# The second attention of a two-layer trunk: TensorE put in the order of the source

## The chip, the cores and the metric

The kernel runs on one core of one Trainium2 chip. The core has a matrix engine (TensorE, PE in the profile; its weight loads are listed apart as PEld), a vector engine (VectorE, DVE), a scalar engine (ScalarE, ACT), a general engine (GpSimd, POOL) and a queue engine that issues transfers (SyncE, SP). Each engine takes its instructions in its own order, and semaphores make one wait for another. The metric is the device time of one execution in microseconds (us).

## The reference, cut to what matters

The model has two layers over 512 latent tokens and 256 context tokens, of width 1024. The change is in the attention of the second layer, which has 16 query heads of 64 columns, 4 key and value heads, a band of 128 tokens to either side, all context keys, and one learned sink logit per head that takes part in the softmax but has no value:

```
q_x, k_x, v_x = jnp.split(h_x @ w_in, [C_Q_COLS, C_Q_COLS + C_KV_COLS], axis=-1)
q_x = apply_rope(heads(q_x, GQA_HEADS), cos, sin)
...
s = jnp.einsum('bqkgd,bnkd->bkgqn', qg, k).astype(jnp.float32) * (HEAD_DIM ** -0.5)
s = jnp.where(mask, s, NEG_INF)
p = jax.nn.softmax(jnp.concatenate([s, sink], axis=-1), axis=-1)[..., :-1]
o = jnp.einsum('bkgqn,bnkd->bqkgd', p.astype(v.dtype), v)
...
out_x = block_sweep(blk, q_x).reshape(B, S, C_Q_COLS) @ w_out
```

In this layer only the latent tokens have queries. After it come the second feed-forward block and a last norm.

## The kernel before

Activations lie transposed: 1024 columns as eight tiles of 128 rows (hb in the profile), each as a high and a low part, so that one product of full precision is three matmuls: high weight by high input, high by low, low by high (`mm3`, lines 207 to 209). A projection of 128 output columns for 512 tokens is therefore 8 x 3 = 24 matmuls of 128x512. Weights come from memory as 128x1024 tiles (raw) and are split: ACT makes the high part (wh, line 158), DVE the low part (wl, line 159).

The stage of the change runs in this order of the source. First the keys of two heads for the latent tokens (`k_x(0)`, 24 matmuls of 128x512), whose inputs the norm has just been making one tile after the other (DVE lines 353 and 355, ACT line 354); then the norm of the context tokens, which begins with two small matmuls (line 312); the values in three groups (`v_part`, lines 432 to 434: 144 matmuls of 128x256); the context keys, the second pair of key heads, and the first query projection. A query projection ends with the rotation of positions (`rope_of`): DVE shuffles and multiplies (lines 386 and 387), POOL multiplies and adds (388 and 389), ACT and DVE write the two parts of gq (369 and 372).

Then come 32 steps: eight pairs of heads m, each with four blocks i of 128 queries. A step has two functions. `a` does the scores: eight matmuls (1540 and 1542) into two buffers s of PSUM, one for each head of the pair, and there are only these two; DVE adds the mask and finds the extreme (1544); ACT exponentiates (1549, with the sum of the row) and takes the exponential of the sink, one head at a time (1551); DVE adds and inverts (1553 and 1554); POOL scales p (1557). `b` turns p by 8 or 10 transposes on TensorE (1569 and 1581), copies them into one buffer pt (ACT 1577 and 1582, DVE 1575), and after every second step does the values of two blocks at once (line 411, ten matmuls that must stay together) and splits their result. `run_steps` calls a of step n, then b of step n-1, then the extra work ("fillers") of step n: the seven query projections that are left, and the half of the output projection that needs the first eight heads only (eight pieces of 12 matmuls, one for each 128 columns of the output). Both have the one PSUM buffer lin. A table says which steps have them: two whole projections in the four steps of m = 0 and of m = 1, one in those of m = 2, 3 and 4, two pieces of the output projection at m = 5, four at m = 6, two at m = 7.

This order of the source is not the order on the engines. A scheduler of the framework reorders every engine's queue when the program is built, by its own costs; only groups marked as unbroken stay together.

After the 32 steps, the other half of the output projection follows (t from lines 207 to 209), and the norm for the feed-forward block.

Of the kernel before, what the change touches and what calls it, by code (L numbers as in the profile page):

```python
# [17 lines left out]
KT = D // P  # L18
# [19 lines left out]
def tile_trunk(  # L38
# [1414 lines left out]
    with ExitStack() as st:  # L1453
# [22 lines left out]

        def k_x(i, w):
# [14 lines left out]

        w0 = [wslice(t) for t in S.next()]
# [14 lines left out]
        def q_piece(m):  # L1508
            def f():
                wh, wl = (wslice(t) for t in S.next())  # L1510
                ps = linp() if m else tp()
                mm3(ps, wh, wl, xh, xl)
                q_tile(m, ps)
            return f
# [10 lines left out]
        def gqa_step(m, i):  # L1525
# [5 lines left out]
            def a():  # L1531
# [4 lines left out]
                for c in range(2):  # L1536
# [13 lines left out]
                    sk = 2 * m + c  # L1550
                    nc.scalar.activation(es[:, c : c + 1], snk[:, sk : sk + 1], AF.Exp, bias=mx[:, c : c + 1], scale=-1.0)
                    pp.append(p)
                nc.vector.tensor_add(rs, rs, es)
# [6 lines left out]
            def b():  # L1560
# [41 lines left out]
            return a, b  # L1602
# [4 lines left out]
        def wo1(m, w, c0, n, k0):  # L1607
            wh, wl = wo_slices(w, m % 2)
            ps = tp() if k0 else linp()
            cs = slice(c0, c0 + n)  # L1610
            if k0:
                before[0] = mm3(ps[:, 0:n], wh, wl, lambda k: hx[k0 + k][:, 0, cs], lambda k: hx[k0 + k][:, 1, cs], 4)
            else:
                mm3(ps.rearrange("p (a n) -> p a n", a=2), wh, wl, lambda k: att(k)[0], lambda k: att(k)[1], 4)
            gate = mod[1][:, 2, 0, m : m + 1]
            if k0 == 0:
                x1[m] = xr[m]
            nc.vector.scalar_tensor_tensor(x1[m][:, cs], ps[:, 0:n], gate, x1[m][:, cs], op0=ALU.mult, op1=ALU.add)

        def first_part(t):  # L1620
            d = {}

            def f(m):
                if m % 2 == 0:
                    d["w"] = S.next()
                wo1(m, d["w"], 0, NX, 0)

            return [lambda m=m: f(m) for m in (2 * t, 2 * t + 1)]

        for m in range(KT):  # L1630
# [3 lines left out]
        q_piece(0)()  # L1634
        steps, fillers = [], []
        plan = {
            0: [q_piece(1), q_piece(2)], 1: [q_piece(3), q_piece(4)], 2: [q_piece(5)], 3: [q_piece(6)], 4: [q_piece(7)],
            5: first_part(0), 6: first_part(1) + first_part(2), 7: first_part(3),
        }
        for m in range(8):  # L1640
            steps += [gqa_step(m, i) for i in range(4)]
            fillers += spread(plan[m], 4)
        run_steps(steps, fillers)
        held = []
        for t in range(4):
            w = S.next(0 if t >= 2 else 2)
            for m in (2 * t, 2 * t + 1):
                if t == 0:
                    wo1(m, w, 0, NX, 4)
                else:  # L1650
                    wo1(m, w, 0, 256, 4)
                    held.append((m, w))
# [3 lines left out]
        sums = sq_sum([x1[k][:, halves[0]] for k in range(KT)], npool)  # L1656
        for m, w in held[:1]:
            wo1(m, w, 256, 256, 4)
# [3 lines left out]
        for m, w in held[1:]:  # L1662
            wo1(m, w, 256, 256, 4)
# [319 lines left out]
```

## Time and profile before

| what | us |
| --- | --- |
| three runs of the kernel | 1601.09, 1604.99, 1609.46 |
| their median | 1604.99 |
| span of the profiled execution | 1606.8 |
| keys, values and first query projection in it | 990.4 to 1033.3 |
| first scores to the last values in it | 1039.4 to 1216.6 |
| TensorE busy in the span | 1541.8 |
| VectorE busy in the span | 1242.9 |

For the profiled execution only its span is given, 1606.8 us; it lies between the runs' lowest and highest time, 1.8 us above their median. In the rows of a timeline the first number is the start in us from the span's beginning, the second the duration. Matmuls overlap in the pipe: the time that one takes from its neighbours is the distance between two starts and not its duration, and "busy" counts the duration.

### The profile page before, as it was taken

Reading aid. Unit: us, or ns where it says so; the run is one execution under the profiler, and the core shown is the slowest. Engines: PE = TensorE matmul, PEld = TensorE weight load, DVE = VectorE, ACT = ScalarE, POOL = GpSimd, SP = SyncE. Lnnn points to the kernel's source line nnn. Section 1 sums busy time; section 2 is a strip of 40 time slices with the busy share of each in tenths; the row PEclk is TensorE's granted clock in tenths of the full one; section 3 lists DMA queues with packets and bytes.
Section 4 is the critical chain, followed back from the end, with each engine's and each line's share of the span. In section 5 each row is a group of like instructions: output and inputs, shape, how many; then the busy total and the mean of one; then the engine's idle time right before and its main releaser. Section 6 shows DMA issues by size and latency. Waiting matters only on the chain.

```text
span 1606.8 us, 25479 instructions
## 1 busy us (share of the span) xinstructions
PE 1541.8 (96%) x9854; PEld 1377.4 (86%) x9854; DVE 1242.9 (77%) x2125; ACT 734.1 (46%) x1276; POOL 275.9 (17%) x311
## 2 busy tenths in 40 slices
PE   5899999999999999999999999999998999999997
PEld 3798888877878998999999998886777899989897
DVE  4667798966698789879798867677766987869686
ACT  4346545445344413434424254466664543525354
POOL 2222223463010000010100001354331000000001
PEclk9999999999999999999999999999999999999999
DMA  9312354543145465485866652320011442423321
GB/s 348 100 53 70 99 157 136 182 128 101 63 132 158 118 173 155 133 221 154 213 183 162 201 146 71 106 66 27 15 40 54 131 144 68 131 72 100 118 80 53
DMA packets 68577, 195.28 MB, mean 122 GB/s; under 512 B 6772, under 2 KB 19220, under 8 KB 68456
## 3 DMA queue, kind: packets, MB, share of 16 engines
q1 hardware_dynamic: 58824, 161.26, 31.5%
q0 software_dynamic: 9056, 31.87, 9.4%
q8 instruction: 78, 1.28, 0.3%
q10 hardware_dynamic: 576, 0.52, 0.1%
q14 instruction: 43, 0.35, 0.1%
HBM read 160.45 MB, written 4.86 MB: 103 GB/s over the span
## 4 chain that ended last, share of the span: by engine, by line
PE 52%; DVE 5%; DMA 4%; issue 4%; ACT 1%; POOL 0%; DVEq 0%; POOLq 0%; ACTq 0%; SPq 0%
PE f L1764 4%; PE f L1763 4%; PE f L1762 4%; PE f L1334 4%; PE f L1333 4%; PE f L1332 4%; PE f L1374 3%; PE f L1375 3%; PE f L1373 3%; PE t L411 2%; PE f L1815 2%; PE f L1817 2%; PE f L1816 2%; DMA wl<-raw 2%; PE t L1569 2%
## 5 line engine op out<-in xcount | busy, mean ns | idle before, releaser
L196 ACT ACTIVATE wh<-raw 128x1024 fp32r<-128x1024 f32 (+1 forms) x96 | 92.3, 978 | 232.4 <-DVE raw L540 106.6
L207 PE MATMUL lin<-hb,wh 128*128 128x512 f32 (+1 forms) x456 | 162.1, 356 | 8.3 <-DVE rbuf L387 2.1
L208 PE MATMUL lin<-hb,wh 128*128 128x512 f32 (+1 forms) x456 | 160.3, 351 | 1.0 <-DVE hb L1106 0.7
L209 PE MATMUL lin<-hb,wl 128*128 128x512 f32 (+1 forms) x456 | 158.4, 347 | 0.0
L197 DVE TENSOR_TENSOR wl<-raw,wh 128x1024 fp32r<-128x1024 f32 (+1 forms) x96 | 107.1, 1122 | 36.3 <-ACT wh L196 34.3
L269 DVE SCALAR_TENSOR_TENSOR junk<-raw,tables 128x1024 bf16<-128x1024 f32 x80 | 98.6, 1233 | 19.2 <-DMA raw<-in_ada_wT_dram 18.7
L202 POOL DMA_DIRECT2D wl<-raw x39 | 34.0, 872 | 445.3 <-ACT wl L201 412.0
L207 PEld LDWEIGHTS lin<-hb,wh 128*128 128x128 f32 x456 | 86.3, 189 | 23.9 <-issue 2.8
L1373 PE MATMUL f<-g,wh 128*128 128x512 f32 (+1 forms) x304 | 103.0, 340 | 0.6 <-DVE s L1362 0.6
L1374 PE MATMUL f<-g,wh 128*128 128x512 f32 (+1 forms) x304 | 102.9, 339 | 0.0
L1763 PE MATMUL f<-hb,wh 128*128 128x256 f32 x360 | 101.8, 284 | 0.0
L1762 PE MATMUL f<-hb,wh 128*128 128x256 f32 x360 | 101.6, 283 | 0.0
L1764 PE MATMUL f<-hb,wl 128*128 128x256 f32 x360 | 101.4, 284 | 0.0
L1375 PE MATMUL f<-g,wl 128*128 128x256 f32 (+1 forms) x304 | 100.8, 337 | 0.0
L1334 PE MATMUL f<-hb,wl 128*128 128x384 f32 x288 | 96.5, 335 | 1.0 <-DMA wl<-raw 1.0
L208 PEld LDWEIGHTS lin<-hb,wh 128*128 128x128 f32 x456 | 86.5, 190 | 12.4 <-DVE hb L1106 1.4
L159 DVE TENSOR_TENSOR wl<-raw,wh 128x1024 fp32r<-128x1024 f32 x61 | 80.7, 1325 | 20.6 <-ACT wh L158 20.3
L1332 PE MATMUL f<-hb,wh 128*128 128x384 f32 x288 | 96.4, 335 | 0.0
L1333 PE MATMUL f<-hb,wh 128*128 128x384 f32 x288 | 96.4, 335 | 0.0
L209 PEld LDWEIGHTS lin<-hb,wl 128*128 128x128 f32 x456 | 86.5, 190 | 10.8
L158 ACT CAST wh<-raw 128x1024 fp32r<-128x1024 f32 x61 | 63.9, 1048 | 67.0 <-PE t L208 15.0
L339 POOL TENSOR_TENSOR ns_a<-ns_a,ns_s 128x256 f32<-128x256 f32 (+1 forms) x16 | 17.9, 1118 | 433.7 <-ACT ns_s L335 427.0
(395 smaller groups left out, 4851.3 us busy)
## 6 DMA issues: line engine op xcount, KB each, us to landing
raw<-in_w_dram SPq DMA_DIRECT2D x132, 512.0 KB, 3.7
raw<-in_ada_wT_dram SPq DMA_DIRECT2D x80, 512.0 KB, 3.8
wl<-raw POOLq DMA_DIRECT2D x39, 512.0 KB, 6.3
raw<-in_w_ab_dram SPq DMA_DIRECT2D x24, 512.0 KB, 4.2
raw<-in_ada_w_dram SPq DMA_DIRECT2D x16, 512.0 KB, 9.5
raw<-in_w_c_dram SPq DMA_DIRECT2D x12, 512.0 KB, 4.4
nb<-in_na_bias_dram POOLq DMA_DIRECT2D x16, 256.0 KB, 3.2
raw<-in_wo_ab_dram SPq DMA_DIRECT2D x8, 512.0 KB, 3.7
```

The lines of the kernel that those rows point to most:

```text
L207: nc.tensor.matmul(ps, wh(k), xh(k), start=k == 0, stop=False)
L208: nc.tensor.matmul(ps, wh(k), xl(k), start=False, stop=False)
L209: end = nc.tensor.matmul(ps, wl(k), xh(k), start=False, stop=k == n - 1)
L1332: nc.tensor.matmul(ps, wh(k), b[:, 0, :], start=k == 0, stop=False)
L1333: nc.tensor.matmul(ps, wh(k), b[:, 1, :], start=False, stop=False)
L1334: nc.tensor.matmul(ps, wl(k), b[:, 0, :], start=False, stop=k == 3)
L1373: nc.tensor.matmul(ps, hi, g[:, 0, cols[v]], start=first, stop=False)
L1374: nc.tensor.matmul(ps, hi, g[:, 1, cols[v]], start=False, stop=False)
L1375: nc.tensor.matmul(ps, lo, g[:, 0, cols[v]], start=False, stop=last)
L1762: nc.tensor.matmul(ps, wh(k), b[:, 0, :], start=k == 0, stop=False)
L1763: nc.tensor.matmul(ps, wh(k), b[:, 1, :], start=False, stop=False)
L1764: nc.tensor.matmul(ps, wl(k), b[:, 0, :], start=False, stop=k == 3)
```

## The change

Four things are done.

1. From the first key projection up to the sums before the next norm, TensorE's queue is taken from the scheduler (`manual_schedule` for PE alone) and stands in the order of the source. The other engines are still ordered by the scheduler.
2. The step loop is new. In iteration n stand the scores of step n, the values of step n-2, the fillers, and the transposes of step n-1.
3. A query projection is cut into three pieces of 9, 9 and 6 matmuls, and a piece of the output projection into two of 6. The 21 pieces of the queries are spread over steps 0 to 17, the 16 of the output projection over steps 18 to 31. The first query projection stays whole and ahead of the loop.
4. The two exponentials of the sink become one: DVE subtracts the sink logits from the extremes of both heads (128x2), ACT takes one exponential of 128x2.

```diff
+        by_hand = st.enter_context(ExitStack())
+        by_hand.enter_context(tc.manual_schedule(engines={mybir.EngineType.PE}))
         w0 = [wslice(t) for t in S.next()]
         k_x(0, w0)
...
+        def in_parts(begin, ps, h, l, cuts, done, cols=slice(0, NX), n=KT):
...
+            def f(c):
+                if c == 0:
+                    d["w"], d["ps"] = begin(), ps()
+                o, (wh, wl) = d["ps"][:, cols], d["w"]
+                for k in range(cuts[c], cuts[c + 1]):
+                    nc.tensor.matmul(o, wh(k), h(k), start=k == 0, stop=False)
+                    nc.tensor.matmul(o, wh(k), l(k), start=False, stop=False)
+                    nc.tensor.matmul(o, wl(k), h(k), start=False, stop=k == n - 1)
+                if c == len(cuts) - 2:
+                    done(d["ps"])
...
-                    sk = 2 * m + c
-                    nc.scalar.activation(es[:, c : c + 1], snk[:, sk : sk + 1], AF.Exp, bias=mx[:, c : c + 1], scale=-1.0)
                     pp.append(p)
+                nc.vector.tensor_sub(es, mx, snk[:, 2 * m : 2 * m + 2])
+                nc.scalar.activation(es, es, AF.Exp)
                 nc.vector.tensor_add(rs, rs, es)
...
+            def b2():
+                h = i % 2
                 if h == 0:
                     return
+                pt = turned[0]
                 o = tp()
...
-        q_piece(0)()
...
-        run_steps(steps, fillers)
+        for f in q_piece(0):
+            f()
+        steps = [gqa_step(m, i) for m in range(8) for i in range(4)]
+
+        fillers = spread([f for m in range(1, 8) for f in q_piece(m)], 18) + spread([f for t in range(4) for f in first_part(t)], 14)
+        for n in range(len(steps) + 2):
+            if n < len(steps):
+                steps[n][0]()
+            if n > 1:
+                steps[n - 2][2]()
+            for f in fillers[n] if n < len(fillers) else []:
+                f()
+            if 0 < n <= len(steps):
+                steps[n - 1][1]()
...
         sums = sq_sum([x1[k][:, halves[0]] for k in range(KT)], npool)
+        by_hand.close()
```

Three places show how the rows move. The first is TensorE at the start of the stage, where hb_124 to hb_131 are the eight tiles of the normed latent tokens, L207 to L209 with 128x512 are the first keys and L432 to L434 are the values. Before:

```order
L207 MATMUL t<-hb_124,wh 128x512
L432 MATMUL t<-wh,hb_124 128x256 x2
L208 MATMUL t<-hb_124,wh 128x512
L209 MATMUL t<-hb_124,wl 128x512
L207 MATMUL t<-hb_125,wh 128x512
L433 MATMUL t<-wh,hb_124 128x256
L434 MATMUL t<-wl,hb_124 128x256
```

After:

```order
L207 MATMUL t<-hb_124,wh 128x512
L208 MATMUL t<-hb_124,wh 128x512
L209 MATMUL t<-hb_124,wl 128x512
L207 MATMUL t<-hb_125,wh 128x512
L208 MATMUL t<-hb_125,wh 128x512
L209 MATMUL t<-hb_125,wl 128x512
```

Before, the matmuls of two blocks of the values stand between those of the keys, 44 in all up to the last one of the keys; in the changed kernel all 24 of the keys stand first, then the two matmuls of the context norm, then the values.

The second is TensorE where the first query projection (t) ends. Before, the whole second query projection (lin) follows, and the first scores come behind it:

```order
L208 MATMUL t<-hb_131,wh 128x512
L209 MATMUL t<-hb_131,wl 128x512
L207 MATMUL lin<-hb_124,wh 128x512
L208 MATMUL lin<-hb_124,wh 128x512
L209 MATMUL lin<-hb_124,wl 128x512
```

After (lines 1486 to 1488 are now the three matmuls, 1556 and 1558 the scores):

```order
L1487 MATMUL t<-hb_131,wh 128x512
L1488 MATMUL t<-hb_131,wl 128x512
L1556 MATMUL s<-gk_9440,gq 128x256
L1556 MATMUL s<-gk_9441,gq 128x256
L1558 MATMUL s<-gk_9440,gq 128x256
```

The scores now follow the first query projection with nothing between them; 18 matmuls of the second stand behind the first scores.

The third is TensorE near the end of the loop. Before, there is a step without a filler, transposes straight after transposes and scores after values:

```order
L1569 MATMUL t<-ident,p 128x128 x8
L1581 MATMUL t<-ident,p 128x128 x2
L1540 MATMUL s<-gk_9440,gq 128x256
L1540 MATMUL s<-gk_9441,gq 128x256
L1542 MATMUL s<-gk_9440,gq 128x256
L1542 MATMUL s<-gk_9441,gq 128x256
L411 MATMUL t<-pt,gv 64x256 x6
L411 MATMUL t<-pt,gv 64x128 x2
L411 MATMUL t<-pt,gv 64x256 x2
L1540 MATMUL s<-gk_9440,gq 128x256
```

After:

```order
L411 MATMUL t<-pt,gv 64x256 x6
L411 MATMUL t<-pt,gv 64x128 x2
L411 MATMUL t<-pt,gv 64x256 x2
L1486 MATMUL lin<-hb_128,wh 128x512
L1487 MATMUL lin<-hb_129,wh 128x512
L1488 MATMUL lin<-hb_128,wl 128x512
L1486 MATMUL lin<-hb_130,wh 128x512
L1487 MATMUL lin<-hb_131,wh 128x512
L1488 MATMUL lin<-hb_130,wl 128x512
L1585 MATMUL t<-ident,p 128x128 x8
L1597 MATMUL t<-ident,p 128x128 x2
```

Every iteration has a piece of a projection between the values and the transposes.

More of the change, by code (lines that the diff above doesn't have):

```diff
@@ L1474, in q_tile @@
             evac_pair(qs[m], 0, NX, rope_of(ps, gp), -0.125)
+        def in_parts(begin, ps, h, l, cuts, done, cols=slice(0, NX), n=KT):
+            d = {}
+            def f(c):
[8 more added lines that the diff above has]
+                    done(d["ps"])
+            return [lambda c=c: f(c) for c in range(len(cuts) - 1)]
         def k_x(i, w):
@@ L1508, in q_piece @@
         def q_piece(m):
[L1509 to L1514, printed above, removed]
+            return in_parts(
+                lambda: [wslice(t) for t in S.next()], linp if m else tp, xh, xl, (0, 3, 6, KT), lambda ps: q_tile(m, ps)
+            )
         def att(m):
```

50 lines of the change are left out of this document (24 added, 26 removed).

## The prediction

> **What bounds the kernel now.** I read the page first, for the share of each engine, then the stretches of the stage, then TensorE's waits, then its timeline.
>
> ```profile
> PE 1541.8 (96%) x9854; PEld 1377.4 (86%) x9854; DVE 1242.9 (77%) x2125; ACT 734.1 (46%) x1276; POOL 275.9 (17%) x311
> ```
>
> TensorE bounds the whole. The table by stretches has, after the times, busy us of PE, PEld, DVE, ACT and POOL, then the granted clock.
>
> ```profile
> 990.00:1004.20 14.20, 13.60 (x73) 11.99 (x74) 13.75 (x24) 8.60 (x15) 0.34 (x1) 0.88 0.25 80
> 1039.30:1112.00 72.70, 69.28 (x397) 55.72 (x398) 54.63 (x116) 41.82 (x98) 38.13 (x34) 0.95 0.17 53
> 1112.00:1156.00 44.00, 41.13 (x302) 32.05 (x302) 33.63 (x83) 31.84 (x86) 15.65 (x20) 1.00 0.04 13
> 1156.00:1190.00 34.00, 34.00 (x231) 27.97 (x230) 23.97 (x53) 18.98 (x48) 11.57 (x12) 1.00 0.15 44
> 1190.00:1216.60 26.60, 22.62 (x180) 16.71 (x178) 15.70 (x44) 17.64 (x50) 8.79 (x12) 1.00 0.02 6
> 1039.30:1216.60 177.30, 167.04 (x1105) 132.45 (x1105) 127.94 (x295) 110.29 (x280) 74.14 (x78) 0.98 0.11 34
> ```
>
> The step loop is the last row. TensorE is not idle at all where pieces of the output projection fill the steps (1156 to 1190), and loses most where steps have none (1112 to 1156, 1190 to 1216.6) and around 1100, where the clock falls too. DVE is busy 72% of the loop. TensorE's waits in the loop (us in total, times, longest):
>
> ```profile
> PE s L1540 <- ACT p L1549: 7.3, 10, 1.3
> PE t L411 <- DVE pt L1575: 1.2, 3, 0.9
> PE lin L207 <- DVE rt L387: 1.1, 2, 0.7
> ```
>
> The largest is that for a score buffer, which the exponential has to release. Since busy counts overlapping durations, I measure what the loop's work takes by starts in the saturated stretch. One pair of steps there, from values to values:
>
> ```profile
> 1161.37 2.17 PE L411 MATMUL t<-pt,gv 128*64 128x256 f32 x20
> ...
> 1165.57 0.39 PE L207 MATMUL lin<-hb,wh 128*128 128x512 f32 x1
> ...
> 1168.33 1.04 PE L1569 MATMUL t<-ident,p 128*128 128x128 f32 x8
> ...
> 1170.38 0.40 PE L207 MATMUL lin<-hb,wh 128*128 128x512 f32 x1
> ...
> 1173.22 2.17 PE L411 MATMUL t<-pt,gv 128*64 128x256 f32 x20
> ```
>
> The pair takes 11.85 us. Its 24 filler matmuls take 2.76 + 2.84 = 5.60, 0.233 each; the attention of a pair is the other 6.25. The loop has 16 pairs, 100.0 us, and 7 x 24 + 8 x 12 = 264 fillers, 61.5 us: **161.5 us** if TensorE never waits. Before, the second projection (24 x 0.233 = 5.6) is already done when the loop begins, so 155.9 us of work take 177.2: about 21 us are lost, and these are what the change can win.
>
> **The change part by part.**
>
> *The start of the stage loses.* Before, the matmuls of the values fill TensorE while the norm delivers the inputs of the first keys.
>
> ```profile
> 990.39 0.51 PE L207 MATMUL t<-hb,wh 128*128 128x512 f32 x1 [1.49 <-ACT hb L354]
> ...
> 994.96 1.43 PE L312 MATMUL lin<-res,ones 128*128 128x256 f32 x4
> 996.04 0.58 PE L207 MATMUL t<-hb,wh 128*128 128x512 f32 x1
> ...
> 1003.93 0.40 PE L209 MATMUL t<-hb,wl 128*128 128x512 f32 x1
> ...
> 1007.87 0.28 PE L432 MATMUL t<-wh,hb 128*128 128x256 f32 x1
> 1007.99 0.28 PE L433 MATMUL t<-wh,hb 128*128 128x256 f32 x1
> ```
>
> The keys end at 1003.93 + 0.23 = 1004.2 with 44 matmuls of the values done; these are worth 44 x 0.12 = 5.2 us and come after the keys now. What comes earlier is the keys' end. DVE makes the last input:
>
> ```profile
> 998.11 0.42 DVE L317 TENSOR_SCALAR ns_v<-lin 128x256 f32<-128x256 f32 x1
> ...
> 1001.76 0.75 DVE L355 SCALAR_TENSOR_TENSOR hb<-norm,mod,hb 128x512 fp32r<-128x512 f32 x1
> ```
>
> Line 317 and two like it (320, 321), each 0.42 long and about 0.33 from start to start, move behind it, since the context norm now starts after the keys. So the last input is there at 1002.5 - 1.0 = 1001.5, two matmuls follow, and the keys end at 1002.0. The two matmuls of line 312 come next (1.1 us by their distance to the row after them). From 1004.2 to the end of the first query projection, 1033.3, the queue was full but for 0.5 us. After: 1002.0 + 1.1 + 29.1 - 0.5 + 5.2 = 1036.9, **3.6 us later**.
>
> *The first scores lose their cover.* Before, the second projection ran through the rotation of the first:
>
> ```profile
> 1033.06 0.39 PE L209 MATMUL t<-hb,wl 128*128 128x512 f32 x1
> 1033.52 0.75 DVE L386 STREAM_SHUFFLE ru<-t 128x512 f32<-128x512 f32 x1
> 1034.42 1.29 POOL L388 TENSOR_TENSOR ru<-ru,tables 128x512 f32<-128x512 f32 x1 [5.68 <-DVE ru L386]
> 1035.78 2.15 POOL L389 TENSOR_TENSOR rt<-rt,ru 128x512 f32<-128x512 f32 x1
> 1037.97 1.28 ACT L369 ACTIVATE gq<-rt 64x512 fp32r<-64x512 f32 x2 [3.65 <-POOL rt L389]
> 1038.63 1.40 DVE L372 SCALAR_TENSOR_TENSOR gq<-rt,gq 64x512 fp32r<-64x512 f32 x2 [1.85 <-ACT gq L369]
> 1039.37 0.51 PE L1540 MATMUL s<-gk,gq 128*128 128x256 f32 x2 [0.48 <-DVE gq L372]
> ```
>
> That chain is 6.1 us from 1033.3. Now nothing stands behind the projection but the scores, so TensorE idles 6.1 us and the loop begins at 1036.9 + 6.1 = 1043.0, with the second projection still to do (it is in the 161.5).
>
> *The clock.* Idle time lowers it:
>
> ```profile
> 992.00:996.00 4.00, 4.00 (x17) 3.58 (x16) 3.96 (x7) 3.01 (x4) 0.00 (x0) 0.57 0.11 43
> 1102.00:1104.00 2.00, 1.91 (x6) 1.62 (x7) 2.00 (x6) 0.55 (x3) 1.79 (x1) 0.50 0.00 0
> ```
>
> A mean of 0.57 over 4 us is 3.4 us at half speed, which is 1.7 us of work lost. I charge 1.7 for the start of the loop; bounds 0 and 5 (three such stretches, the third at the start of the stage where TensorE is now used less than half of the time). The Trainium skill (TensorE: Matmul & The Clock Gate, "What's actually happening") says that the clock falls after an idle window of about 3.4 us and needs about 3.4 us of steady work to return: by that an idle stretch of 6 us costs the same 1.7, but frequent short idling, its section "A second HAM failure mode", would keep bringing it back, which no stretch of the loop here shows except around 1102.
>
> *The loop gains.* Durations for its chain, from the groups within the loop:
>
> ```profile
> L1544 DVE CUSTOM_DVE_ANT_0 s<-s,gm,snk 128x640 f32<-128x640 f32 x32 | 28.1, 886 | 2.6 <-PE s L1542 2.5
> L1549 ACT ACTIVATE p<-s,mx 128x640 f32<-128x640 f32 x32 | 25.4, 795 | 14.9 <-DVE mx L1544 7.8 <-DVE rs L1554 3.2 <-POOL p L1557 2.4
> L1551 ACT ACTIVATE es<-snk,mx 128x1 f32<-128x1 f32 x64 | 18.0, 286 | 0.6 <-DVE rs L1554 0.6
> L1553 DVE TENSOR_TENSOR rs<-rs,es 128x2 f32<-128x2 f32 x32 | 6.8, 212 | 9.7 <-ACT es L1551 9.2 <-ACT p L1549 0.5
> L1557 POOL TENSOR_SCALAR p<-p,rs 128x640 f32<-128x640 f32 x32 | 26.9, 852 | 46.4 <-DVE rs L1554 39.7 <-PE s L1542 3.8 <-ACT pt L1577 3.0
> L1575 DVE COPY pt<-t 128x512 f32<-128x512 f32 x32 | 22.0, 687 | 5.3 <-PE t L1569 5.2
> ```
>
> After the scores of step n, both heads' exponentials are done at about 2.2 us (the second reduction ends at 1.35, the exponential 0.8 later). The shortest way to the next scores is a step without values in the second half: 6 fillers, 1.4, and transposes, 0.9 to 1.1; the buffer of the second head is wanted after half of the next scores, at 2.9. It fits by 0.7, without any wait on ACT or DVE. Scaled p comes at about 2.2 + 0.3 (sink) + 0.4 (sum, inverse) + 2 x 0.85 = 4.9 with the hops; the transposes of step n start after the fillers of iteration n+1: 6.8 us of work in between (2 x 1.4 + 1.0 + 0.9 + 2.1). It fits by 1.9. The values, two iterations behind, want pt copied: the DVE copy (0.69) has the 0.9 us of scores in between. It just fits, and waits about 0.1 us in 16 iterations, 1.6 in all. Before, the values waited for that copy too, 1.2.
>
> What does not fit: in iteration 12 the last piece of one projection and the first of the next stand together, and the one lin buffer is read by lines 386 and 387 first: 0.75 + 0.69 and a hop, 1.6 us. In each of six more projections ACT's write of gq waits for POOL (2.15 + 1.29 behind line 386) with exponentials queued behind it on ACT, and scores behind these: I take 0.2 each, 1.3 in all. Sum of **waits in the loop: 4.5 us**. Bounds: 1.6, the lin wait alone, as TensorE idles nowhere from 1156 to 1190 either, and 14, two thirds of what the loop loses now, were the order as bad in its filled steps as the old one in its bare ones.
>
> The sinks: 64 x 0.286 = 18 us of ACT become 32 x 0.286, and DVE gets 32 x 0.21 = 7 us more: DVE (127.94 + 7) of some 172 us, 78%. Both lie under TensorE's work; the chain loses 0.286 on ACT and gains none, as DVE subtracts while ACT still exponentiates. Nothing on the path. If that cover went, it would be 0.2 us a step.
>
> *The end.* The last step has no filler: transposes wait about 0.5, values about 1.0 for the copies, **1.5 us**; bounds 1 and 2. What follows the loop stands in the same order as before on TensorE and SP.
>
> Sum: 1043.0 + 161.5 + 1.7 + 4.5 + 1.5 = 1212.2, against the values' end before:
>
> ```profile
> 1214.46 2.17 PE L411 MATMUL t<-pt,gv 128*64 128x256 f32 x20 [0.88 <-DVE pt L1575]
> 1216.56 0.51 PE L207 MATMUL t<-hb,wh 128*128 128x512 f32 x1
> ```
>
> The gain is 4.4 us. The span of 1606.8 lies 1.8 above the median of the runs; taken off the median, 1604.99, it gives **1600.6**, say 1601. With all low bounds it is 1604.99 - 9.5 = 1595.5, with all high ones 1604.99 + 9 = 1614.
>
> **The rivals.** A measurement can tell 0.5% here, 8 us: below 1597 is faster, above 1613 slower.
>
> *The loop runs without any wait and pulls the start along.* For it: the saturated stretch, and DVE's 78%. Then the waits go to 1.6, the clock stays up, the end is 1.0: 1595.5; if the start also loses less than 3.6, because DVE's norm runs ahead with less in its queue, 1593. Against: two idle stretches before the loop are certain.
>
> *The fixed order makes waits that the scheduler went round.* TensorE can no longer take other work while its first instruction waits. Place: scores of step n+1 behind an exponential that sits behind gq on ACT, in steps 0 to 17, and short steps of 18 to 31. Price: 0.6 us a step, the middle of the ten waits for p now (7.3 / 10 = 0.7), on 32 steps is 19 instead of 4.5: 1604.99 - 4.4 + 14.7 = 1615. It decides the sign from 4.5 + 4.4 = 8.9 us of waits, 0.28 a step. Against: the fillers now stand exactly between the steps that waited.
>
> *The clock halves again and again in the loop.* Three more stretches of 3.4 us, 1.7 each, and the gain is gone: 1606. For it: the fall at 1102, behind the longest wait, 1.3 us. Against: 1112 to 1156 has waits and the clock at 1.00.
>
> **How the numbers follow.** Forecast 1601 with its own range 1596 to 1606: 0.5. First rival, 1593 to 1596: 0.27. Second, 1615: 0.15. Third, 1606: 0.08. Faster by over 0.5%: 0.27 and a tenth of the forecast, 0.32; slower 0.15; within 0.53. The range 1592 to 1612 leaves out most of the second rival and a little below.
>
> **What would show it.** The keys ending near 1002 with values after them and the first query projection near 1037; one idle stretch of about 6 us before the first scores, with the clock at half behind it; scores to values in about 169 us; waits of scores for p under 3 us and one of lin for line 387 near 1.5. If scores wait for p in most steps, the second rival is right; if the stage's start keeps its time, my first term is wrong.

## The result, and the profile after

The changed kernel is slower: **1615.69 us** in the median of four runs (1614.8 to 1617.07), against 1605.73 for the kernel before, a ratio of 1.0064 with a 95% interval of 1.0044 to 1.0084. The forecast was 1601, and 1612 the upper end of its range.

The profiled execution has a span of 1615.2 us. What lies behind the last values takes the same in both (1615.2 - 1224.99 = 390.2 after, 1606.8 - 1216.56 = 390.2 before), and what lies ahead of the stage differs by a few us from one kernel's profile to the next although nothing there was changed. So I measure the **stage**, from the first key matmul to the first matmul behind the last values. These are rows of TensorE's timeline after: three of the keys (the first matmul, the one behind the last but one input, the last), the two matmuls of line 312, which leave four records, the end of the first query projection, the first scores, the last values and what follows:

```profile
988.50 0.50 PE L207 MATMUL t<-hb,wh 128*128 128x512 f32 x1 [1.50 <-ACT hb L354]
...
999.26 0.80 PE L208 MATMUL t<-hb,wh 128*128 128x512 f32 x1 [0.42 <-DVE hb L355]
...
1001.13 0.63 PE L209 MATMUL t<-hb,wl 128*128 128x512 f32 x1
1001.56 1.24 PE L312 MATMUL lin<-res,ones 128*128 128x256 f32 x4
...
1036.37 0.39 PE L1488 MATMUL t<-hb,wl 128*128 128x512 f32 x1
1042.61 0.80 PE L1556 MATMUL s<-gk,gq 128*128 128x256 f32 x2 [5.85 <-DVE gq L372]
...
1222.89 2.17 PE L411 MATMUL t<-pt,gv 128*64 128x256 f32 x20 [0.93 <-DVE pt L1591]
1224.99 0.50 PE L207 MATMUL t<-hb,wh 128*128 128x512 f32 x1
```

The stage took 1216.56 - 990.39 = 226.2 us before and takes 1224.99 - 988.50 = **236.5** now, 10.3 more; it began 1.9 earlier, so the span grew by 8.4. The prediction asked for 226.2 - 4.4 = 221.8. It is short by 14.7 us, and these are what has to be explained.

The table by stretches of the changed kernel (columns as in the prediction's table) shows where they lie. The last row is the step loop.

```profile
1040.00:1060.00 20.00, 14.63 (x69) 12.08 (x69) 13.14 (x29) 9.02 (x20) 8.26 (x7) 0.84 0.17 54
...
1100.00:1120.00 20.00, 16.63 (x106) 13.34 (x105) 14.76 (x35) 10.85 (x25) 9.41 (x10) 1.00 0.09 27
...
1160.00:1180.00 20.00, 20.00 (x140) 16.70 (x139) 14.88 (x40) 11.85 (x33) 7.89 (x11) 1.00 0.09 28
```

```profile
1042.61:1224.99 182.38, 171.04 (x1128) 138.69 (x1129) 136.02 (x326) 100.54 (x248) 72.65 (x78) 0.98 0.11 33
```

From 1160 to 1200 TensorE is never idle, as the prediction wanted for the whole loop. The holes are at its beginning (1040 to 1060), and between 1100 and 1160, where projections of queries end and are rotated; short ones follow in the last steps. TensorE's waits in the changed kernel, from 1030 to 1230:

```profile
PE s L1556 <- DVE gq L372: 5.9, 1, 5.9
PE s L1556 <- ACT p L1565: 3.5, 6, 1.5
PE t L1585 <- POOL p L1573: 3.5, 4, 2.1
PE t L411 <- DVE pt L1591: 2.0, 2, 1.0
PE lin L1486 <- DVE rt L387: 1.4, 1, 1.4
```

The first is the uncovered rotation ahead of the loop. The wait of transposes for POOL's scaled p is new; before it was

```profile
PE t L1569 <- POOL p L1557: 0.2, 1, 0.2
```

**How one such hole comes about.** The changed kernel around 1105, on GpSimd, ScalarE, VectorE and TensorE in this order:

```profile
1103.33 2.16 POOL L389 TENSOR_TENSOR rt<-rt,ru 128x512 f32<-128x512 f32 x1
```

```profile
1105.52 1.28 ACT L369 ACTIVATE gq<-rt 64x512 fp32r<-64x512 f32 x2 [3.10 <-POOL rt L389]
1106.83 0.79 ACT L1565 ACTIVATE p<-s,mx 128x640 f32<-128x640 f32 x1
```

```profile
1105.06 0.14 DVE L1560 DVE_READ_ACCUMULATOR2_ANT mx<- 128x1 f32 x1
```

```profile
1105.93 0.38 PE L1597 MATMUL t<-ident,p 128*128 128x128 f32 x2
1107.77 0.51 PE L1556 MATMUL s<-gk,gq 128*128 128x256 f32 x2 [1.46 <-ACT p L1565]
```

The extreme that the exponential needs is there at 1105.06 + 0.14 = 1105.2. ScalarE does not start it: the first in its queue is the write of gq, which waits for POOL's addition until 1105.5 and then takes 1.28. The exponential starts at 1106.83, 1.6 us after its input, and the next scores, which need the buffer that it reads, wait 1.46. In truth they wait longer, as the idle time counts only from the end of the last transpose's duration. In the stretch without idle time the scores start 0.14 us behind the same transposes:

```profile
1162.49 0.38 PE L1597 MATMUL t<-ident,p 128*128 128x128 f32 x2
1162.63 0.48 PE L1556 MATMUL s<-gk,gq 128*128 128x256 f32 x2
```

By this distance the hole is 1107.77 - 1105.93 - 0.14 = 1.70, and 0.24 of it is hidden in the busy time.

The longest wait for POOL, 2.12, comes about on VectorE, at the loop's beginning:

```profile
1054.05 1.43 DVE L159 TENSOR_TENSOR wl<-raw,wh 128x1024 fp32r<-128x1024 f32 x1
...
1056.21 0.45 DVE L1569 TENSOR_TENSOR rs<-rs,es 128x2 f32<-128x2 f32 x1
...
1057.38 0.15 DVE L1570 RECIPROCAL rs<-rs 128x2 f32<-128x2 f32 x1
```

```profile
1053.76 0.19 ACT L1568 ACTIVATE es<-es 128x2 f32<-128x2 f32 x1
```

```profile
1057.71 2.42 POOL L1573 TENSOR_SCALAR p<-p,rs 128x640 f32<-128x640 f32 x2 [1.07 <-DVE rs L1570]
```

The sink exponential is done at 1053.95, but the sum and the reciprocal of the row, 0.6 us of work, end only at 1057.5, behind the shuffle and the product of a rotation, a copy, the split of a weight and the extremes of the next step; then POOL scales p, and the transposes start at 1058.98.

### The profile page after: what moved, and what is told of

Read it like the earlier page. It is cut to its first block, busy times and chain, and to the rows that moved or that the text cites. A ratio compares the mean times of both kernels' runs of the same rounds, so it can differ in the third digit from the quotient of the medians.

```text
span 1615.2 us, 25426 instructions
## 1 busy us (share of the span) xinstructions
PE 1539.0 (95%) x9854; PEld 1375.3 (85%) x9854; DVE 1251.1 (77%) x2157; ACT 725.0 (45%) x1244; POOL 270.8 (17%) x311
## 3 DMA queue, kind: packets, MB, share of 16 engines
q8 instruction: 78, 1.28, 0.3%
## 5 line engine op out<-in xcount | busy, mean ns | idle before, releaser
L197 DVE TENSOR_TENSOR wl<-raw,wh 128x1024 fp32r<-128x1024 f32 (+1 forms) x96 | 107.0, 1120 | 37.1 <-ACT wh L196 35.8
L207 PE MATMUL lin<-hb,wh 128*128 128x256 f32 (+1 forms) x368 | 126.6, 345 | 7.4 <-DVE rbuf L387 2.1
L208 PE MATMUL lin<-hb,wh 128*128 128x256 f32 (+1 forms) x368 | 125.2, 340 | 0.9 <-DVE hb L1106 0.6
L209 PE MATMUL lin<-hb,wl 128*128 128x256 f32 (+1 forms) x368 | 123.6, 336 | 0.0
L339 POOL TENSOR_TENSOR ns_a<-ns_a,ns_s 128x256 f32<-128x256 f32 (+1 forms) x16 | 16.8, 1049 | 433.3 <-ACT ns_s L335 426.7
L207 PEld LDWEIGHTS lin<-hb,wh 128*128 128x128 f32 x368 | 69.6, 189 | 19.7 <-issue 2.7
L208 PEld LDWEIGHTS lin<-hb,wh 128*128 128x128 f32 x368 | 69.7, 189 | 9.5 <-DVE hb L1106 1.4
L209 PEld LDWEIGHTS lin<-hb,wl 128*128 128x128 f32 x368 | 69.6, 189 | 7.5
```

Source lines behind the costliest of these rows:

```text
L197: return nc.vector.tensor_sub(lo, src, f32(hi))
L207: nc.tensor.matmul(ps, wh(k), xh(k), start=k == 0, stop=False)
L208: nc.tensor.matmul(ps, wh(k), xl(k), start=False, stop=False)
L209: end = nc.tensor.matmul(ps, wl(k), xh(k), start=False, stop=k == n - 1)
```

## The experiments

The stage and the parts of the loop stand in one table. "Work" is the prediction's price (161.5, or 155.9 where the second projection is done ahead of the first scores), "idle" the loop less TensorE's busy time, "clock" the loop times one less the granted clock (rounded to 0.01, so good to 0.9 us; half clock in idle time is in it too), "rest" what then remains. The kernel before took 1605.70, 1604.07 and 1605.08 us in the three groups of runs, 1 to 4, 5 to 8 and 9 to 12, each group on a chip of its own; each ratio is against its own group. The numbers of the runs are those of the texts below.

| kernel | us | ratio, 95% interval | stage | loop | work | idle | clock | rest |
| --- | --- | --- | --- | --- | --- | --- | --- | --- |
| before | 1605.73 | | 226.2 | 177.2 | 155.9 | 10.2 | 3.5 | 7.6 |
| changed | 1615.69 | 1.0064 (1.0044 to 1.0084) | 236.5 | 182.4 | 161.5 | 11.3 | 3.6 | 5.9 |
| 1: order fixed later | 1610.67 | 1.0044 (1.0031 to 1.0057) | 230.0 | 181.8 | 161.5 | 11.5 | 3.6 | 5.2 |
| 2: second projection ahead | 1608.32 | 1.002 (1.0012 to 1.0029) | 231.8 | 177.7 | 155.9 | 11.5 | 3.6 | 6.8 |
| 3: both | 1605.15 | 1.0005 (0.9994 to 1.0016) | 225.0 | 176.7 | 155.9 | 11.3 | 1.8 | 7.7 |
| 4: no fixed order | 1598.78 | 0.9967 (0.9955 to 0.998) | 219.7 | 170.7 | 155.9 | 7.9 | 0 | 6.9 |
| 5: 3, gq later | 1597.61 | 0.9956 (0.9941 to 0.9971) | 219.4 | 170.5 | 155.9 | 6.6 | 1.7 | 6.3 |
| 6: 3, no rotation | 1598.26 | 0.9962 (0.9947 to 0.9978) | 218.7 | 169.7 | 155.9 | 7.1 | 0 | 6.7 |
| 7: before, one sink exponential | 1604.43 | 0.9998 (0.9989 to 1.0007) | 225.8 | 177.5 | 155.9 | 10.2 | 5.3 | 6.0 |
| 8: 4, two sink exponentials | 1597.03 | 0.9951 (0.9934 to 0.9968) | 217.4 | 169.0 | 155.9 | 6.6 | 0 | 6.5 |
| 9: changed, gq later | 1610.60 | 1.0038 (1.0026 to 1.005) | 231.9 | 177.7 | 161.5 | 7.1 | 3.6 | 5.5 |
| 10: 4, gq later | 1608.64 | 1.0027 (1.0014 to 1.0041) | 228.6 | 180.2 | 155.9 | 12.8 | 1.8 | 9.7 |
| 11: 5, values one back | 1638.83 | 1.0213 (1.0197 to 1.0228) | 258.9 | 210.5 | 155.9 | 33.6 | 14.7 | 6.3 |
| 12: 5, whole pieces | 1630.29 | 1.0159 (1.0144 to 1.0174) | 249.2 | 200.2 | 155.9 | 26.0 | 12.0 | 6.3 |

Three rows of the table of stretches from which this is worked out, of the loops of runs 4, 11 and 12 in this order (PE busy behind the length, the granted clock third from the end):

```profile
1038.29:1208.99 170.70, 162.79 (x1104) 130.25 (x1104) 134.49 (x326) 102.48 (x248) 73.34 (x78) 1.00 0.12 36
```

```profile
1035.16:1245.67 210.51, 176.87 (x1104) 140.84 (x1104) 139.75 (x326) 100.39 (x248) 71.81 (x78) 0.93 0.09 29
```

```profile
1037.38:1237.58 200.20, 174.16 (x1104) 136.88 (x1104) 133.61 (x326) 101.41 (x248) 73.80 (x78) 0.94 0.10 31
```

For run 4: idle 170.70 - 162.79 = 7.9, clock nothing, rest 162.79 - 155.9 = 6.9.

**Runs 1 to 3: the start of the stage.** Run 1 fixes the order only from the loop on, so that the scheduler again lays values between the keys; run 2 does the whole second query projection ahead of the first scores; run 3 does both.

```diff
-        by_hand = st.enter_context(ExitStack())
-        by_hand.enter_context(tc.manual_schedule(engines={mybir.EngineType.PE}))
         w0 = [wslice(t) for t in S.next()]
...
             f()
+        by_hand = st.enter_context(ExitStack())
+        by_hand.enter_context(tc.manual_schedule(engines={mybir.EngineType.PE}))
         steps = [gqa_step(m, i) for m in range(8) for i in range(4)]
```

```diff
-        for f in q_piece(0):
-            f()
+        for m in range(2):
+            for f in q_piece(m):
+                f()
...
-        fillers = spread([f for m in range(1, 8) for f in q_piece(m)], 18) + spread([f for t in range(4) for f in first_part(t)], 14)
+        fillers = spread([f for m in range(2, 8) for f in q_piece(m)], 18) + spread([f for t in range(4) for f in first_part(t)], 14)
```

> The changed kernel with TensorE's fixed order beginning only behind the first query projection, so that keys, values and that projection are ordered by the scheduler as before. The changed kernel took 1615.7 us, the one before 1605.7. Theory A (three separate losses: the values no longer fill the making of the first keys, 5.3 us by the two profiles; the first scores wait 5.9 us with nothing behind them, and the clock is at half afterwards; waits in the loop): 1610 to 1611, the query projection ends about 43 us after the first key matmul instead of 48. Rival B (the chain of the softmax on ACT, DVE and POOL sets the loop's pace, so that what is won ahead of it is waited away in it): 1614 to 1616, with the earlier start and a longer loop.

> The changed kernel with the second query projection whole and ahead of the first scores; the other six are spread over steps 0 to 17 in 18 pieces. Theory A: its 5.6 us of matmuls now stand in the 5.9 us of idle time, and the half clock behind that goes too (2 us): 1608. Rival B: the loop has 24 fillers less to hide its chain, so its steps wait more and little is won: 1613 to 1616.

> The last two together. Theory A: the gains add, 1615.7 - 5 - 7.5 = 1603, some 2 to 3 us under the kernel before, with the loop's waits as they are. Rival B: 1612 to 1616.

Measured: 1610.7, 1608.3 and 1605.2 us; the stage is shorter by 6.4, 4.7 and 11.5. The two losses at the start are real, and they add up: 6.4 + 4.7 = 11.1 against 11.5. Mending both brings the kernel to the time of before, and no further, 2 us short of what was expected of run 3. The loop of run 3 takes 176.7 with the same work as that of before in 177.2: the new loop, in its fixed order, gains nothing. Its largest wait, 7.3 us, is that for p, to the tenth the one that the kernel before had:

```profile
PE s L1554 <- ACT p L1563: 7.3, 8, 2.1
```

**Run 4: no fixed order.** The changed source, with the scheduler left to order TensorE.

```diff
         by_hand = st.enter_context(ExitStack())
-        by_hand.enter_context(tc.manual_schedule(engines={mybir.EngineType.PE}))
```

> The changed source (new loop, cut projections, values two steps back, one exponential for the sinks) with no fixed order at all: the scheduler orders TensorE too, and its rows show it putting the cut projections together again in runs of 18 to 24 and the second one ahead of the first scores. Theory A: the start and the first scores are as before and the loop's losses are those before: 1603 to 1607, no change against the kernel before. Rival B' (the new loop itself is worse, whoever orders it): 1612 or more.

Measured: 1598.8 us, below every number that was expected, and faster than the kernel before. The scheduler lays the second projection ahead of the first scores and values between the keys, as before; its loop takes 170.7, 6 us less than the fixed order with the same work (run 3). The waits in its loop:

```profile
PE s L1555 <- ACT p L1564: 4.0, 6, 1.1
```

No wait for POOL is left, none is longer than 1.2, and the clock stays at 1.00 in the loop. So the new source of the loop is worth 226.2 - 219.7 = 6.5 us of the stage under the scheduler, 3.5 of it by the clock, and the fixed order takes 16.8 (236.5 - 219.7) away.

**Runs 5, 6 and 9: the write of gq.** Run 5 is run 3 with the write of gq an iteration later in the source, and ScalarE's half of it bound to stand behind the sink exponential of the next step; run 9 is the same edit in the changed kernel itself. Run 6 is run 3 without the rotation of the queries m = 2 to 7: DVE's shuffle and POOL's two operations are left out and gq is written from a product of DVE, so its output is another.

```diff
-            nc.scalar.activation(dst[a, j, c], src[a, :], AF.Copy, scale=scale)
+            with tc.issue_after(after.ins) if after else nullcontext():
+                nc.scalar.activation(dst[a, j, c], src[a, :], AF.Copy, scale=scale)
...
-            evac_pair(qs[m], 0, NX, rope_of(ps, gp), -0.125)
+            t = rope_of(ps, gp)
+            if m < 2:
+                evac_pair(qs[m], 0, NX, t, -0.125)
+            else:
+                late.append(lambda: evac_pair(qs[m], 0, NX, t, -0.125, last_es[0]))
...
-                nc.scalar.activation(es, es, AF.Exp)
+                last_es[0] = nc.scalar.activation(es, es, AF.Exp)
...
                 steps[n - 2][2]()
+            now, late[:] = late[:], []
+            for f in now:
+                f()
```

> The third experiment's kernel (start ordered by the scheduler, second query projection ahead of the first scores, fixed order from there; 1605.2 us) with one thing moved: on ACT, the write of gq that waits for POOL's rotation is issued behind the sink exponential of the following step and not ahead of that step's exponentials. The work is the same. Theory A (the loop's waits come from ACT's queue, where gq waits about 3 us for POOL with exponentials behind it): of the 7.3 us that scores wait for p, about 5 go: 1600. Rival B (DVE and POOL set the pace, ACT's order does not matter, the wait only moves to the transposes or the copies): 1604 to 1606.

Run 6:

```diff
-            evac_pair(qs[m], 0, NX, rope_of(ps, gp), -0.125)
+            if m < 2:
+                t = rope_of(ps, gp)
+            else:
+                t = gp.tile([P, NX], F32, tag="rt", name="rt", bufs=2)
+                nc.vector.tensor_mul(t, ps, cost)
+            evac_pair(qs[m], 0, NX, t, -0.125)
```

> The third experiment's kernel with the rotation of the query projections 2 to 7 left out but for DVE's multiplication: no shuffle on DVE (0.75 us each), no multiplication and addition on POOL (3.4 us each), so gq does not wait for POOL; the queries are not rotated and the output is another. Theory A: the waits for p fall by as much as in the run before or more, 1598 to 1601. Rival B: it frees POOL and little of DVE, the waits for p stay above 5 us in all, 1603 or more.

> The changed kernel as it is (fixed order from the first query projection on, second projection not ahead of the first scores), with one edit: ScalarE's write of the query's lower half (gq) is issued behind the next step's sink exponential instead of at the end of the rotation. Theory (ScalarE's order is a loss of its own, some 7 us, as it was where fixed order and second projection had been mended): 1607 to 1609 us. Rival (in the changed kernel the ramp and VectorE's order hide that gain, so that another wait ends just as late): 1612 us or more.

Measured: 1597.6 us for run 5, 1598.3 for run 6 (0.9962, interval 0.9947 to 0.9978, its stage 218.7), 1610.6 for run 9 (whose fixed order begins with the first keys, as in the changed kernel, and not, as the expectation has it, with the first query projection). The edit shortens the stage by 5.6 us in run 3 and by 4.6 in the changed kernel. Run 9 lies between what its two theories asked for: the gain is there, but nearer to 5 than to 7. The wait of scores for p falls from the 7.3 of run 3 to 3.7 in run 6 and in run 5 to

```profile
PE s L1561 <- ACT p L1570: 3.6, 6, 2.1
```

That leaving the rotation out altogether (run 6) brings hardly more than mending only ScalarE's order (run 5) shows that the order, and not POOL's time, is what costs. In run 9 the rows that answer to those quoted above are

```profile
1105.14 0.80 ACT L1572 ACTIVATE p<-s,mx 128x640 f32<-128x640 f32 x1 [3.01 <-DVE mx L1567]
...
1107.27 1.28 ACT L370 ACTIVATE gq<-rt 64x512 fp32r<-64x512 f32 x2
```

```profile
1106.08 0.50 PE L1563 MATMUL s<-gk,gq 128*128 128x256 f32 x2
...
1107.35 0.50 PE L1563 MATMUL s<-gk,gq 128*128 128x256 f32 x2 [0.53 <-ACT p L1572]
```

The exponential starts 1.7 us earlier than in the changed kernel, gq is written behind it and the scores go on with a wait of 0.53 in place of 1.46 and 0.52. The waits of run 9 in the loop:

```profile
PE t L1592 <- POOL p L1580: 1.7, 1, 1.7
...
PE s L1563 <- ACT p L1572: 1.2, 4, 0.5
```

The wait for p fell from 3.5 to 1.2 and, with it, that for POOL from 3.5 to 1.7, as POOL scales what the late exponential delivers.

**Runs 7 and 8: the sinks.** Run 7 is the kernel before with the one sink exponential and nothing else; run 8 is run 4 with two exponentials of 128x1 again.

```diff
-                    sk = 2 * m + c
-                    nc.scalar.activation(es[:, c : c + 1], snk[:, sk : sk + 1], AF.Exp, bias=mx[:, c : c + 1], scale=-1.0)
                     pp.append(p)
+                nc.vector.tensor_sub(es, mx, snk[:, 2 * m : 2 * m + 2])
+                nc.scalar.activation(es, es, AF.Exp)
```

> The kernel before with only the sinks' exponentials joined (DVE subtracts 128x2, ACT takes one exponential). The prediction's term: nothing on the path, 1605 to 1606. Rival C (ACT is what releases the score buffers, and 0.29 us less of it in each of 32 steps is felt where steps have no filler, 12 of them, and shifts the others): 1600 to 1602, which would be most of what the fourth experiment won (1598.8).

> The fourth experiment's kernel (new loop, no fixed order, 1598.8 us) with two sink exponentials of 128x1 again as before. If the spreading of the fillers is what it won: 1599 to 1600. Rival C (the sinks won it): 1604 to 1606.

Measured: 1604.4 us, ratio 0.9998 (0.9989 to 1.0007), stage 225.8; and 1597.0, ratio 0.9951 (0.9934 to 0.9968), stage 217.4. In the loop of run 7 the new subtraction and the one exponential take

```profile
L1551 DVE TENSOR_TENSOR es<-mx,snk 128x2 f32<-128x2 f32 x32 | 6.8, 213 | 0.6
L1552 ACT ACTIVATE es<-es 128x2 f32<-128x2 f32 x32 | 6.4, 201 | 5.0 <-DVE es L1551 5.0
```

against 18.0 us of ScalarE before, and the time does not move: all of it lies under TensorE's work. With the sinks out, what makes runs 4 and 8 faster than before is the rest of the loop's new source: the distance of the values, the cut pieces and their spread. Which of these does it was not separated; the scheduler puts many of the cut pieces together again (24, 24 and 23 matmuls in the first steps of run 4).

**Run 10: gq later without the fixed order.**

```diff
         by_hand = st.enter_context(ExitStack())
-        by_hand.enter_context(tc.manual_schedule(engines={mybir.EngineType.PE}))
...
+                late.append(lambda: evac_pair(qs[m], 0, NX, t, -0.125, last_es[0]))
```

> The changed source without its fixed order (the kernel that took 1598.8) and with the write of gq issued behind the next step's sink exponential. Theory (even where the scheduler orders TensorE, the exponentials wait behind that write): 1594 to 1597 us. Rival (the scheduler had already gone round it, there is nothing left to gain): 1598 to 1600 us.

Measured: 1608.6 us, so neither: it costs 10 where both theories saw a gain or nothing. The scheduler orders TensorE anew (its queue differs from that of run 4 from the third step on), and the waits for POOL are back:

```profile
PE t L1591 <- POOL p L1579: 3.8, 4, 1.7
PE s L1562 <- ACT p L1571: 3.5, 6, 0.8
```

Idle time in the loop rises from 7.9 to 12.8 us. Which of its other moves brought that I did not separate; it stays open. What the run shows is that the edit's gain with the fixed order did not carry over to the kernel in which the scheduler orders TensorE.

**Runs 11 and 12: what covers the softmax in a fixed order.** Both start from run 5. Run 11 does the values one iteration after their scores, right behind the transposes, in place of two; run 12 leaves the projections whole, six of the queries over steps 0 to 17 and eight pieces of the output projection over the rest.

```diff
-        for n in range(len(steps) + 2):
+        for n in range(len(steps) + 1):
...
-            if n > 1:
-                steps[n - 2][2]()
...
                 steps[n - 1][1]()
+                steps[n - 1][2]()
```

```diff
-                ..., xh, xl, (0, 3, 6, KT), lambda ps: q_tile(m, ps)
+                ..., xh, xl, (0, KT), lambda ps: q_tile(m, ps)
...
-                    lambda k: att(k)[0], lambda k: att(k)[1], (0, 2, 4), lambda ps, m=m: done(m, ps), slice(0, 2), 4,
+                    lambda k: att(k)[0], lambda k: att(k)[1], (0, 4), lambda ps, m=m: done(m, ps), slice(0, 2), 4,
```

> The kernel that took 1597.6 (both start mends, gq behind the sink exponential), with the values right behind the transposes of their own step, one turn of the loop back and not two. Theory (the distance of two turns is what hides the copies of the turned weights): values wait for the copies about 1 us in most of 16 pairs, 1606 to 1614 us. Rival (the copies are hidden by other work at either distance): 1597 to 1600 us.

> The kernel that took 1597.6, with its projections uncut: six whole query projections spread over the turns 0 to 17, eight whole output projections over the rest. Theory (small pieces in each turn are what covers the softmax of the turn; turns without any stand bare for 2 to 3 us again): 1602 to 1608 us. Rival (an even spread is enough, cut or whole): 1597 to 1599 us.

Measured: 1638.8 and 1630.3 us, 41 and 33 more than run 5 and far above what was expected. In a fixed order much of the loop's time hangs on both parts, the distance of the values and the cut pieces. The waits in the loop of run 11 and of run 12:

```profile
PE t L1590 <- POOL p L1578: 11.7, 5, 2.8
PE t L412 <- DVE pt L1596: 10.7, 9, 1.9
PE t L412 <- DVE rs L1574: 5.2, 5, 1.6
```

```profile
PE s L1561 <- ACT p L1570: 13.7, 11, 2.0
PE t L1590 <- POOL p L1578: 8.6, 6, 3.5
```

Run 11 has the waits for copies that were expected (9 of about 1.2), and others that weren't: between 1112 and 1120, for instance, row sums and copies stand on DVE behind the split of a weight and a write of gq, 1.92 us each, so POOL's scaling, the next transposes and the values all come late. And with 33.6 and 26.0 us of idle time the clock falls: by the table it takes 14.7 and 12.0 us, where run 5 lost 1.7, about a third of what each lost.

## Why the prediction was wrong

The loop's gain did not come. The prediction charged the start with 3.6 + 5.6 + 1.7 = 10.9 us (the later end of the first projection, the second projection that no longer lies under the rotation, the clock) and had the loop, for the same 155.9 us of work, fall from 177.2 to 155.9 + 4.5 + 1.5 = 161.9. Mending the start (run 3) gives 11.5 back, so that charge was nearly right; but the loop of run 3 takes 176.7. Of a gain of 15.3 us 0.5 was there. In place of the 6.0 us of waits its row of the table has 11.3 us of idle time, 1.8 of clock and a rest of 7.7.

The 14.7 us that are missing in the stage, by the prediction's own terms:

| term | predicted | measured | difference |
| --- | --- | --- | --- |
| first key matmul to first scores | 1043.0 - 990.39 = 52.6 | 1042.61 - 988.50 = 54.1 | 1.5 |
| clock in the loop | 1.7 | 3.6 | 1.9 |
| waits in the loop, with its end | 4.5 + 1.5 = 6.0 | 11.3 | 5.3 |
| the loop's work, rest | 161.5 | 161.5 + 5.9 | 5.9 |

Their sum is 14.6; the tenth is rounding.

*"The start of the stage loses" was right in kind and too small.* The first query projection was to end 3.6 us later, counted from the first key matmul; it ends 5.2 later (48.1 us against 42.9). The difference lies in the keys: they take 13.1 us from the first one, not 11.6. The sum gave the matmuls at the end of the keys full speed. After 999.26 they stand 0.43 apart instead of 0.23, at half clock: five intervals make 1.0 us. About 0.5 more is the last input, which is there 11.6 us behind the first key matmul (DVE's last operation ends at 1000.1) and not 11.1. I had put this stretch into the upper bound of the clock and not into the sum.

*"The first scores lose their cover" was right*: one wait of 5.9 us for gq, 6.1 predicted. Run 2, which puts the cover back, shortens the stage by 4.7.

*"The clock" was mis-sized by half.* I charged one stretch of half clock. There are two: from 1039.5 to 1046.4 behind the idle rotation, and from 1060.0 to 1063.4 behind the 2.12 that the transposes wait (rows of both are quoted in the last section). The rule of the Trainium skill (TensorE: Matmul & The Clock Gate, "What's actually happening") asks for about 3.4 us of steady work until the clock is back. The first stretch agrees: scores start at 1042.61 and the clock returns 3.75 us later. But some 3 us of half clock lay in idle time and cost nothing, so that the loss is one of work under half clock, 1.9 us there and 1.7 at the second. The idle window of about 3.4 us by which the prediction had the clock fall does not fit the second: the holes around its beginning are of 2.12 and 0.55.

*"Waits in the loop, 4.5" was the step that failed most.* Its lin wait is right (1.4 for 1.6) and its wait for pt copies (2.0 for 1.6 and the end's 1.0) as well. The six writes of gq, taken at 0.2 each, were mis-sized: mending them alone is worth 4.6 us (run 9) or 5.6 (run 5), so 0.7 to 0.9 for each of its seven or six writes, against 1.3 in all. The prediction had the mechanism, in this term and in its second rival, but the 0.2 rests on no row, and the rival's 0.6 on waits of the kernel before, in which the scheduler had gone round them. The other part is the transposes' wait for scaled p, 3.5 us, put at nothing by "it fits by 1.9": that margin was worked out with every engine free, and the rows at the loop's beginning show DVE's other work ahead of the row sum. Some of it followed the late exponentials, since run 9 halves it (3.5 to 1.7).

*"161.5 if TensorE never waits" was nearly right, but "about 21 us are lost" says nothing of what they are.* What the table leaves beyond work, idle time and clock is 5.9 us in the changed kernel, 7.6 in the one before and 5.2 to 9.7 in all the others, however their loops are ordered. Part of it is waits: each hole hides 0.07 to 0.25 us in the busy time, as at 1107.77. Worked out like there, for the 17 of the 19 holes whose two matmuls also follow each other without one, that is an estimated 2.8 us in the changed kernel (in the one before, 3.9 us at 20 of 21). So the waits in its loop are about 14 us and not 11.3, against the 6.0 predicted. The other 3 us of the rest I did not find. What of the 21 us can be won is not shown either: the shortest loop here, that of run 8, won 8.

*The second rival* (waits that the scheduler went round, 1615) is the nearest to what came: for the loop it asks for 169.2 + 14.7 = 183.9 us, and 182.4 were measured. It had gq ahead of the exponentials as the place, and that is shown (runs 5 and 9), and run 4 shows that the scheduler's own order has fewer waits. But its price was 0.6 us in each of 32 steps, and by its sign scores would wait for p in most steps. They wait six times, 3.5 us in all; the rest are other waits and the clock. So its time is in part luck.

*The third* (the clock halves again) came once in the loop, not three times. *The sinks at nothing* was right (run 7).

Of the signs named, keys near 1002, the first query projection near 1037, one idle stretch of about 6 with half clock behind it and a lin wait near 1.5 all came; the first two by luck, since the stage began 1.9 us earlier than before, which hides that both came some 1.5 us late within it. Scores to values took 182.4 and not 169, and the waits for p were 3.5.

Two versions do best, and beat both kernels: the changed source without its fixed order and with two sink exponentials (1597.0, 0.9951, interval 0.9934 to 0.9968), and the fixed order from the loop on with the second projection ahead and gq behind the exponentials (1597.6, 0.9956, interval 0.9941 to 0.9971). Their intervals overlap; which is better isn't settled.

## What to carry to other kernels

Fixing one engine's order by hand fixes also what that order doesn't cover: before it replaces a scheduler's, list what the scheduler had put into each stretch in which this engine waits (here values between the keys, 6.4 us, and a projection under the rotation, 4.7), and look at the queues of the other engines for a write that waits for a third engine ahead of work on the chain (4.6). Before a loss is counted as a gain to come, say which wait or which lowered clock each part of it is: of 21 us of loss here, the fixed order won back almost none. And try a change of several parts one part at a time: the new loop was worth 6.5 us under the scheduler, and the fixed order hid it.

## What the runs showed of the hardware

**Idle time costs more than itself, and no hole need be long.** In each trace all changes of the granted clock lie on a grid of 3.41 us: from one change to the next it is 3.41 us or a multiple. Rows cut on this grid (PE busy behind the length, the granted clock third from the end), of run 11 around two waits:

```profile
1112.10:1115.51 3.41, 1.84 (x9) 1.18 (x7) 3.41 (x7) 0.50 (x1) 1.01 (x1) 1.00 0.11 17
1115.51:1118.92 3.41, 1.31 (x8) 0.84 (x8) 2.44 (x9) 2.78 (x8) 2.89 (x4) 1.00 0.39 137
1118.92:1122.33 3.41, 2.56 (x14) 1.81 (x16) 0.71 (x2) 0.00 (x0) 0.67 (x1) 0.50 0.00 0
1122.33:1125.75 3.42, 3.42 (x15) 2.47 (x12) 0.89 (x2) 0.38 (x1) 0.00 (x0) 0.50 0.00 0
```

An idle stretch of 2.8 us, 1.3 us of work and another idle 1.7 are followed by 6.8 us of half clock, which cost 3 us of work. The clock falls behind the piece of the grid in which TensorE was busy for 1.31 of 3.41 us (38%), and not behind the one ahead of it (54%). In the changed kernel:

```profile
1042.94:1046.36 3.42, 3.42 (x13) 3.03 (x13) 2.13 (x6) 1.56 (x5) 0.00 (x0) 0.50 0.03 8
...
1056.60:1060.01 3.41, 0.91 (x6) 0.42 (x4) 3.31 (x7) 2.91 (x6) 2.33 (x3) 1.00 0.39 149
1060.01:1063.42 3.41, 3.23 (x16) 3.01 (x16) 1.95 (x6) 1.05 (x3) 1.69 (x3) 0.50 0.00 0
...
1104.38:1107.79 3.41, 1.95 (x15) 1.53 (x13) 3.17 (x8) 2.22 (x5) 1.11 (x1) 1.00 0.50 154
```

Here 27% busy brings the fall at 1060.01, and 57%, with the hole of 1.46, does not. Laid over the 14 traces of this case from 980 to 1260 us, the grid has 35 falls, each behind a piece that was busy for 52% or less, and 1067 pieces at full clock without a fall, each busy for 52% or more but for one of 43% (run 1, from 1028.6). The clock came back behind pieces that were busy for 84% or more and stayed at half behind those of 82% or less. So each fall brought 3.41 us at half clock or a multiple, and each 3.41 cost up to 1.7 us of work.

The loss in the loop therefore goes by how the holes lie and not by their sum: by the table it is nothing at 7.9 us of idle time (run 4), 3.6 at 7.1 (run 9, where one of two stretches comes from the idle rotation ahead of the loop), 1.8 at 12.8 (run 10) and 14.7 at 33.6 (run 11).

**A stage of unchanged code moves by several us.** The first key matmul starts between 983.4 (run 7) and 991.1 us (run 3) in profiles of kernels whose text up to there is the same. A difference of a few us between two spans says nothing by itself; the stage's own length did.
